# An encoder trunk on one core: the build orders its instructions by a timeline simulation in place of simple clocks

## The chip, the core and the metric

The kernel runs on one core of a Trainium2 chip. A core has five engines that each take a list of instructions in order: PE (TensorE, matrix multiplications; the loads of its weights are shown apart as PEld), DVE (VectorE), ACT (ScalarE), POOL (GpSimd) and SP (SyncE). Here SP does nothing but issue DMAs, the loads from memory into the core; POOL issues most stores and a few loads and does little else. An engine waits on semaphores for the others. The metric is the device time of one execution in microseconds.

## What is computed

The reference is one inference step of a trunk of two layers on 1024 new frames of one stream (the prompt) and 16 frames of each of 8 running streams (the sample), together T = 1152 tokens of width 1024. Layer 0 mixes with stick-breaking attention (8 heads of 64) beside a gated depthwise convolution of width 31; layer 1 mixes with attention over a band of chunks with a learned relative bias. Each layer ends in an MLP with a squared ReLU. All is in 32-bit floats.

```python
# layer 0, mixer (prompt; the sample also has cached k, v and u)
q, k, v, a, g = split(rmsnorm(x, g1) @ w_in)
u = a * sigmoid(g)
z = einsum(q, k) * HEAD_DIM ** -0.5
log_keep = where(mask, log_sigmoid(-z), 0)
between = cumsum(log_keep, reverse=True) - log_keep
w = where(mask, exp(log_sigmoid(z) + between), 0)
c = silu(layernorm(depthwise_conv(u, dw_w) + dw_b))
x = x + concat(w @ v, c) @ w_out
# layer 1, mixer
x = x + softmax(q @ k * scale + bias, in band) @ v @ w_out
# both layers
x = x + square(relu(rmsnorm(x, g2) @ w_up)) @ w_down
```

The outputs are the last layer's normed x, the new keys and values of both layers, and the last 30 rows of u.

## The kernel before

Activations lie transposed, channels on the partitions: a tile is 128 channels by tokens, the width 1024 is KC = 8 such tiles, and the tokens go through PE in three groups of G = 384 (the third holds the last 256 prompt tokens and the 128 of the sample). A 32-bit product is made of three matmuls: each operand is split into a high part, rounded by ACT (L180), and a low part, the rest, by DVE (L181), and high·high, high·low and low·high are summed (SPLIT, in `dense`, L208 to L222, whose matmul is L220). `load_split` (L190) loads 512 columns of a weight into a staging tile (`staging`, L185 to L187, tag st, three buffers) and splits it.

PE's results go to 8 banks of PSUM. The names of tiles in the order and in the trace follow the code: f20 is the bank of gate or value weight 2 and token group 0.

**Start** (`start`, within L674 to L806). The gate and value weights of the first two convolution chunks, numbered 0 to 3 (wf00 to wf31: weight, half), the tokens (x00 to x21: group, piece) and the states of the convolution (u0, u1, L631) are loaded on SP's queue. `ready` splits the weights (hl_wf for weights 0 and 1, hf for 2 and 3), `halves` the tokens (h0, L1543 and L1544), `squares` sums their squares (accs, L291 and L294), ones-matmuls of these (ms_h, L258) and a diagonal matmul (rr_h, L280) bring the row scale of the norm, and `sums` makes the banks f00 to f32. DVE's evacuations L636, L638 and L651 gate them into u0 to u3. The projections of q, k and v follow, whose weights are staged as st_wi; the cached keys of the sample come as ct00k to ct03k (L474).

**Mixer of layer 0.** For each pair of heads q, k, v are projected (psp, psa, psg), then for each block of queries scores z (L864 to L867), on ACT their exponentials, on DVE the reverse cumulative product (kp, L847, a scan along the keys) and its product with the gates (sg, L849), transposes on PE (tpa, L392), splits of these (wha on ACT, wla on DVE), products with v (ava, L404) and a sum (cpa, L414) that is stored to a buffer in memory, cat_d (L361). The sample's streams have the same steps with names in zs, kps, sgs. The convolution is 31 taps (`tap`, L655 to L675) for each of four chunks of channels, on DVE: y = u·w + y, one instruction for the prompt's 1024 tokens and one for the sample's 128; the last tap writes u, which goes to cat_d (L674, L675). The taps are steps of their own that a function `level` spreads between the attention's. `conv_norm` (L935) then loads that back as yl (L955, on POOL's queue), takes the mean by a matmul (mu, L961), subtracts it (L963) and normalizes. The output projection (psoa) follows per 128 channels (wo0a), with the residual in xo, stored as xm_d (L1028).

**MLP.** Up: um (L1380), squared ReLU (L1386 to L1390), stored as hid_d; down: hidden tiles are loaded as hrm, split (hsm), multiplied (pd, L1485), and added on DVE to sl (L1489). **Mixer of layer 1** runs pair by pair of heads: psc (L220), tpc (L392), avc (L404), psoa.

What sets the order: the Python code calls the instructions in an order that `merge` and `level` make from lists of steps with costs written into the code. The build then collects them and its scheduler decides the list of each engine anew, within the dependences; a few are tied by hand (taps come only after the weights step last named, L664). By default the scheduler keeps one simple clock for each engine.

```python
    with tile.TileContext(nc) as tc:
        tile_trunk(tc, ins, outs)
```

## Time and profile before

| | us |
|---|---|
| median of 3 runs | 2881.78 (2876.07 to 2883.00) |
| profiled execution | 2879.29 |
| its span on the core | 2877.5 |
| mean granted PE clock in it | 0.987 |

The span is the time from the first to the last instruction on the core. Times in the traces are us from its start. The stages lie at about: start 0 to 68, mixer of layer 0 to 474, convolution norm and output projection to 667, MLP to 1405, mixer of layer 1 to 1940, its end to 2110, MLP and final norm to 2877.

In a row of a timeline stand start, time taken, engine, line, operation, tile written and tiles read, and in brackets how long the engine had been idle and what ended that. In a row of a stage table stand the stretch, its length, the busy time of each engine with its number of instructions, the granted clock of PE as a share of full speed, the mean share of the core's DMA engines in use and GB/s.

### The profile page before, as it was taken

The page shows a single profiled execution, that of the slowest core. Times are in us where ns is not written, and L with a number is a line of the kernel's source. Part 1 is how long each engine was busy: PE and PEld are TensorE (multiplying, and loading weights), DVE is VectorE, ACT ScalarE, POOL GpSimd, SP SyncE. Part 2 cuts the span into 40 slices and gives each one's busy share as a digit, 9 for nine tenths or more (in the row PEclk, how much of TensorE's full clock was granted, in tenths as well). Part 3 has the DMA queues.
Part 4 walks back from the last instruction along what each step waited for, and adds up shares of the span by engine and source line. Part 5 has one row for each costly group of instructions (what it writes and reads, how often), then busy time and mean ns, then how long its engine had stood idle before and what let it go on. Part 6 is the DMA issues. An engine that isn't in the chain of part 4 may idle for free.

```text
span 2877.5 us, 48092 instructions
## 1 busy us (share of the span) xinstructions
PE 2778.7 (97%) x18586; PEld 2674.3 (93%) x18586; DVE 2015.6 (70%) x3939; ACT 1264.4 (44%) x2644; POOL 282.3 (10%) x511
## 2 busy tenths in 40 slices
PE   8988988899999999999999999998999999999998
PEld 8987876799999999999999999997999999999998
DVE  8999999988666654444567777778786666644445
ACT  5344446665555531211355555556555554411112
POOL 1000101031000000000111111110310110000001
PEclk9999998999999999999999999999999999999999
DMA  4434346443332362321344444446532322732311
GB/s 152 131 102 127 114 123 205 147 162 117 106 105 94 131 232 77 109 79 46 107 141 133 135 143 139 134 132 220 180 123 94 102 99 102 251 102 67 110 34 66
DMA packets 136004, 357.70 MB, mean 124 GB/s; under 512 B 21232, under 2 KB 44976, under 8 KB 133728
## 3 DMA queue, kind: packets, MB, share of 16 engines
q1 hardware_dynamic: 105936, 252.06, 27.5%
q0 software_dynamic: 29696, 102.56, 10.5%
q8 instruction: 146, 2.39, 0.3%
q14 instruction: 82, 0.67, 0.1%
q10 hardware_dynamic: 144, 0.02, 0.0%
HBM read 252.90 MB, written 89.03 MB: 119 GB/s over the span
## 4 chain that ended last, share of the span: by engine, by line
PE 75%; DVE 16%; ACT 4%; issue 3%; DMA 2%; POOL 0%; DVEq 0%; SPq 0%; ACTq 0%; POOLq 0%
PE pd L1485 28%; PE um L1380 23%; PE psc L220 10%; DVE y L671 4%; DVE kp L847 2%; PE avc L404 2%; PE psoa L220 2%; PE tpc L392 2%; PE f L220 1%; DVE sg L849 1%; PE zc L1137 1%; DVE wla L181 1%; PE zc L1138 1%; PE psp L220 1%; PE zs L505 1%
## 5 line engine op out<-in xcount | busy, mean ns | idle before, releaser
L1489 DVE TENSOR_TENSOR sl<-sl,pd 128x384 f32<-128x384 f32 x384 | 211.6, 552 | 342.4 <-PE pd L1485 342.0
L220 PE MATMUL psc<-h,hl_wc 128*128 128x384 f32 x1728 | 328.2, 340 | 0.0
L220 PEld LDWEIGHTS psc<-h,hl_wc 128*128 128x128 f32 x1728 | 298.5, 189 | 13.4 <-issue 11.5
L1380 PE MATMUL um<-sl,hl_m 128*128 128x288 f32 x1548 | 240.3, 296 | 0.0
L1380 PEld LDWEIGHTS um<-sl,hl_m 128*128 128x128 f32 x1548 | 217.7, 188 | 0.0
L671 DVE SCALAR_TENSOR_TENSOR y<-u,dw,y 128x1024 f32<-128x1024 f32 (+1 forms) x232 | 176.4, 807 | 0.4
L220 PE MATMUL psp<-h,hl_wi 128*128 128x384 f32 x864 | 169.7, 345 | 0.2 <-ACT kps L896 0.2
L220 PEld LDWEIGHTS psp<-h,hl_wi 128*128 128x128 f32 x864 | 150.4, 191 | 6.4 <-issue 4.9
L1485 PE MATMUL pd<-hsm,wdm 128*128 128x384 f32 x864 | 150.8, 334 | 0.0
L1485 PEld LDWEIGHTS pd<-hsm,wdm 128*128 128x128 f32 x864 | 149.9, 188 | 0.0
L181 DVE TENSOR_TENSOR hl_m<-xr,hl_m 128x512 fp32r<-128x512 f32 x132 | 92.4, 700 | 57.1 <-ACT hl_m L180 55.8
L180 ACT ACTIVATE hl_m<-xr 128x512 fp32r<-128x512 f32 x132 | 82.2, 623 | 104.7 <-PE um L1380 83.2
L1387 ACT ACTIVATE hdm<-hdm 128x288 f32<-128x288 f32 x192 | 84.8, 442 | 91.7 <-DVE hdm L1386 90.9
L1380 PE MATMUL um<-sl,hl 128*128 128x288 f32 x756 | 119.4, 296 | 0.0
L1104 ACT ACTIVATE s<-s,mxc 128x640 f32<-128x640 f32 (+4 forms) x128 | 88.8, 694 | 59.8 <-DVE mxc L1101 58.1
L1380 PEld LDWEIGHTS um<-sl,hl 128*128 128x128 f32 x756 | 106.6, 188 | 0.8
L180 ACT ACTIVATE wdm<-st_wd 128x512 fp32r<-128x512 f32 x40 | 23.8, 624 | 171.2 <-PE pd L1485 144.8
L1101 DVE CUSTOM_DVE_ANT_0 s<-zc,bp 128x384 f32<-128x384 f32 (+3 forms) x128 | 66.0, 517 | 38.9 <-PE zc L1138 38.1
L180 ACT ACTIVATE whc<-tpc 128x512 fp32r<-128x512 f32 (+1 forms) x144 | 72.5, 523 | 47.0 <-PE tpc L392 46.1
L181 DVE TENSOR_TENSOR wlc<-tpc,whc 128x512 fp32r<-128x512 f32 (+1 forms) x144 | 83.5, 595 | 12.8 <-ACT whc L180 10.4
L1390 POOL DMA_DIRECT2D hid_d<-hdm x96 | 51.9, 540 | 412.9 <-ACT hdm L1388 334.7
L180 ACT ACTIVATE hl<-st_wd 128x512 fp32r<-128x512 f32 x20 | 12.6, 629 | 171.0 <-PE pd L1485 155.3
(495 smaller groups left out, 6997.6 us busy)
## 6 DMA issues: line engine op xcount, KB each, us to landing
hrm<-hid_d SPq DMA_DIRECT2D x64, 576.0 KB, 5.0
xr<-in_w_up_dram SPq DMA_DIRECT2D x64, 512.0 KB, 3.7
st_wd<-in_w_down_dram SPq DMA_DIRECT2D x128, 256.0 KB, 3.3
hid_d<-hdm POOLq DMA_DIRECT2D x96, 288.0 KB, 2.4
st_wc<-in_w_in_c_dram SPq DMA_DIRECT2D x48, 256.0 KB, 2.7
xm_d<-xo POOLq DMA_DIRECT2D x16, 576.0 KB, 3.5
xr<-xm_d SPq DMA_DIRECT2D x16, 576.0 KB, 4.6
xr_d<-xr POOLq DMA_DIRECT2D x16, 576.0 KB, 3.3
```

The source lines that it names most:

```text
L180: ACT(hi, src, AF.Copy)
L181: return tt(lo, src, f(hi), ALU.subtract)
L220: mm(ps()[:, :G], hl[:, a, at:at + P], act[g][k // 4][b][:, k % 4, :], start=n == 0, stop=n == len(todo) - 1)
L392: nc.tensor.transpose(tp[:, c0 + q * P:c0 + (q + 1) * P], blocks.get(j, tile_q), ident)
L404: mm(st["av"][:, o0:o0 + n], vs[:, j, i].rearrange("p a d -> p (a d)"), src[:, c0:c0 + n], start=st["done"] == 0, stop=st["done"] == nmm - 1)
L671: stt(src if j == CW - 1 else dst, src, wj, dst, ALU.mult, ALU.add)
L1101: nc.vector.tensor_tensor_reduce(s[:, c:c + m], z, b, -1.0, mx, ALU.add, ALU.min, new)
L1104: ACT(s[:, :n], s[:, :n], AF.Exp, bias=mx, scale=-1.0, accum_out=tot)
L1380: mm(banks[b, n][:, :TQ], w[:, a, c * P:c * P + P], combo(key, c)[:, h, n * TQ:n * TQ + TQ], start=k < 3 and c == 0 and i == 0, stop=c == ...
L1387: ACT(y, y, AF.Relu)
L1485: mm(ps[:, :G], w[:, a, c % 4 * P:c % 4 * P + P], hid[NB * j + e][b][:, g * G:g * G + G], start=n == 0, stop=n == 3 * NB - 1)
L1489: tt(xs, xs, ps[:, :G], ALU.add)
```

## The change

The context in which the kernel is built gets a flag. The kernel's code, its tiles, buffers and pools stay as they are.

```diff
-    with tile.TileContext(nc) as tc:
+    with tile.TileContext(nc, schedule_with_timeline_sim=True) as tc:
         tile_trunk(tc, ins, outs)
```

With it the scheduler of the build ranks instructions by a simulation of the whole timeline. The two builds hold the same instructions on each engine; the lists differ in order, and with the order in which waits stand. Of the instructions before, 4928 of 17753 stand elsewhere among their neighbours on PE, 2418 of 3941 on DVE, 1246 of 2503 on ACT, 142 of 516 on POOL and 235 of 599 on SP. In the middle of both MLPs PE's list is the same.

The first place is SP's list at the program's start. Before:

```order
L187 DMA st_wf11_194<-in_w_in_ab_dram 128x512
L187 DMA st_wf20_196<-in_w_in_ab_dram 128x512
L698 DMA x10_229<-in_x_dram 128x768
L698 DMA x11_289<-in_x_dram 128x1152
L187 DMA st_wf21_231<-in_w_in_ab_dram 128x512
L698 DMA x12_291<-in_x_dram 128x1152
L187 DMA st_wf30_330<-in_w_in_ab_dram 128x512
L187 DMA st_wf31_332<-in_w_in_ab_dram 128x512
L698 DMA x20_350<-in_x_dram 128x1920
```

and, behind x21, u0, u1, st_wi4_0, st_wi4_1 and st_wi5_0, the cached keys ct00k00 to ct00k02. With the change, behind the same st_wf11 and x10 to x20:

```order
L698 DMA x21_352<-in_x_dram 128x1152
L631 DMA u0_382<-in_conv_in_dram 128x8x30
L631 DMA u1_389<-in_conv_in_dram 128x8x30
L474 DMA ct00k00_1145<-in_sb_k_dram 128x4x256
L474 DMA ct00k01_1147<-in_sb_k_dram 128x4x256
L474 DMA ct00k02_1149<-in_sb_k_dram 128x4x256
L187 DMA st_wf20_196<-in_w_in_ab_dram 128x512
L187 DMA st_wf21_231<-in_w_in_ab_dram 128x512
L187 DMA st_wf30_330<-in_w_in_ab_dram 128x512
L187 DMA st_wf31_332<-in_w_in_ab_dram 128x512
L187 DMA st_wi4_0_662<-in_w_in_ab_dram 128x512
```

Seven weight loads of 256 KB have moved behind ten loads of tokens, states and keys. PE's list at that place, where f20 is the first bank that needs st_wf20 (split as hf20), reads with the change:

```order
L220 MATMUL f10_233<-h0_70_190,hl_wf11_201 128x384
L220 MATMUL f20_264<-h0_00_159,hf20_258 128x384
L220 MATMUL f20_264<-h0_01_160,hf20_258 128x384
L258 MATMUL ms_h00_316<-ones_74,accs_140 128x1 x3
L220 MATMUL f01_354<-h0_00_159,hl_wf00_156 128x384
L220 MATMUL f01_354<-h0_01_160,hl_wf00_156 128x384
```

Before, all 24 matmuls of f20 stood ahead of ms_h00 and of f01; two of them still do.

The second place is DVE's list around kp100, the first scan of a head of the second pair, in the mixer of layer 0. Before:

```order
L671 SCALAR_TENSOR_TENSOR y2_2348<-u2_1429,dw_77,y2_2348 128x1024
L671 SCALAR_TENSOR_TENSOR y2_2348<-u2_1429,dw_77,y2_2348 128x128
L671 SCALAR_TENSOR_TENSOR y2_2348<-u2_1429,dw_77,y2_2348 128x1024
L671 SCALAR_TENSOR_TENSOR y2_2348<-u2_1429,dw_77,y2_2348 128x128
L414 TENSOR_TENSOR cpa013_2495<-ava013_2388,ata013_2493 64x256
L847 SCALAR_TENSOR_TENSOR kp100_2499<-kp100_2499,ones_74 128x128
```

With the change:

```order
L671 SCALAR_TENSOR_TENSOR u1_389<-u1_389,dw_77,y1_1236 128x1024
L671 SCALAR_TENSOR_TENSOR u1_389<-u1_389,dw_77,y1_1236 128x8x16
L181 TENSOR_TENSOR hl_wi14_0_2578<-st_wi14_0_2576,hl_wi14_0_2578 128x512
L847 SCALAR_TENSOR_TENSOR kp100_2499<-kp100_2499,ones_74 128x128
L668 TENSOR_SCALAR y2_2348<-u2_1429,dw_77,cvec_78 128x1024
L668 TENSOR_SCALAR y2_2348<-u2_1429,dw_77,cvec_78 128x128
```

The first nine pairs of taps of chunk 2, which stood ahead of that scan, now stand behind it: u1's last tap comes just before the scan. Taps lag behind the attention's steps like this from the start of the mixer, by up to about 13 us of tap work, and have caught up at the last scan, kps30.

The third place is POOL's list at the end of the taps, where the last chunk's result u3 goes to cat_d and yl is loaded from there. Before:

```order
L361 DMA cat_d0_109<-cpa202_4248 64x256
L674 DMA cat_d0_109<-u3_2647 128x1024
L675 DMA cat_d0_109<-u3_2647 128x8x16
L361 DMA cat_d0_109<-cpa203_4420 64x256
L819 DMA out_sb_v_dram<-sv03_4306 128x1152
L361 DMA cat_d0_109<-cpa210_4502 64x256
L955 DMA yl00_4667<-cat_d0_109 128x384
L350 DMA l0_745<-l0_745 64x1024
L955 DMA yl01_4668<-cat_d0_109 128x384
```

With the change:

```order
L361 DMA cat_d0_109<-cpa211_4570 64x256
L347 DMA k1_744<-k1_744 64x1024
L350 DMA l1_746<-l1_746 64x1024
L674 DMA cat_d0_109<-u3_2647 128x1024
L675 DMA cat_d0_109<-u3_2647 128x8x16
L361 DMA cat_d0_109<-cpa212_4644 64x256
L955 DMA yl00_4667<-cat_d0_109 128x384
L955 DMA yl01_4668<-cat_d0_109 128x384
L955 DMA yl02_4669<-cat_d0_109 128x384
```

The store of u3 has moved behind four more of the attention's stores and stands right ahead of the yl loads, which depend on it. On DVE u3's last tap has moved with it, from just ahead of the scan kp212 to behind sg217, the last scan of that head, near the end of the stage. At the turn from up to down in the MLPs, SP's list has hidden tiles hrm and pieces of sl ahead of the down weights st_wd, and PE's first down rows (pd) go through seven banks with the first hidden tile before the second tile comes; before, the first bank took the first four tiles before the second bank was opened.

## The prediction

> **What bounds the kernel now.** I read the page first, then a table of busy time by stage, then the waits of PE and DVE inside the stages that are not full, then the timelines around the places where the order differs. The page says how much there is to gain at all:
>
> ```profile
> span 2877.5 us, 48092 instructions
> ...
> PE 2778.7 (97%) x18586; PEld 2674.3 (93%) x18586; DVE 2015.6 (70%) x3939; ACT 1264.4 (44%) x2644; POOL 282.3 (10%) x511
> ...
> PE 75%; DVE 16%; ACT 4%; issue 3%; DMA 2%; POOL 0%; DVEq 0%; SPq 0%; ACTq 0%; POOLq 0%
> ```
>
> The change removes no instruction, so PE's 2778.7 us of matmuls stay. PE is idle for 2877.5 − 2778.7 = 98.8 us, and no order can give back more. The stages show where that idle lies (columns: stretch in us, its length, then busy us of PE, PEld, DVE, ACT and POOL, the granted clock, the DMA share and GB/s):
>
> ```profile
> core 0: us, PE busy (x) PEld busy (x) DVE busy (x) ACT busy (x) POOL busy (x), PEclk, DMA share, GB/s
> 16.00:28.00 12.00, 10.42 (x61) 9.86 (x60) 11.15 (x29) 11.30 (x24) 0.00 (x0) 1.00 0.98 319
> 50.00:68.00 18.00, 18.00 (x95) 17.74 (x94) 15.23 (x28) 6.11 (x14) 1.47 (x2) 0.91 0.24 66
> 68.00:108.00 40.00, 40.00 (x234) 39.97 (x233) 39.81 (x49) 10.42 (x19) 4.65 (x8) 1.00 0.29 76
> 108.00:474.00 366.00, 327.60 (x2316) 283.92 (x2314) 357.19 (x498) 170.28 (x386) 35.64 (x63) 0.95 0.44 131
> 474.00:600.00 126.00, 111.05 (x753) 95.16 (x753) 112.83 (x210) 88.07 (x193) 11.88 (x20) 0.96 0.50 171
> 667.00:1009.00 342.00, 342.00 (x2577) 342.00 (x2576) 231.65 (x447) 180.73 (x391) 33.51 (x62) 1.00 0.32 110
> 1430.00:1940.00 510.00, 501.47 (x3649) 474.63 (x3649) 364.80 (x1014) 269.28 (x618) 62.42 (x144) 1.00 0.44 135
> ```
>
> The first MLP (667 to 1009 is its up half) is full of matmuls; its order on PE changes only at its ends, so it can neither gain nor lose. From 50 to 108 PE is full too. From 108 to 474, the stick-breaking mixer with the convolution beside it, DVE is the bound: 357.2 of 366 us, 8.8 idle, while PE waits 38.4. From 474 to 600 neither is full (PE idle 15.0, DVE 13.2): chains of short steps. The second mixer (1430 to 1940) has 8.5 us of PE idle in 510. So the order can matter in the first 50 us, in the DVE-bound stage, and at the seams.
>
> **The first term: the third and fourth gate weights come later.** The order shows that on SP's list the loads of st_wf20, st_wf21, st_wf30, st_wf31 and the first three st_wi move behind the tokens x10 to x21, the convolution states u0 and u1, and three 512-KB key-cache loads ct00k. Before, SP ran them so:
>
> ```profile
> 9.13 0.33 SPq L187 DMA_DIRECT2D st_wf<-in_w_in_ab_dram  x1
> ...
> 13.38 0.84 SPq L187 DMA_DIRECT2D st_wf<-in_w_in_ab_dram  x2
> ...
> 20.16 5.00 SPq L187 DMA_DIRECT2D st_wi<-in_w_in_ab_dram  x3
> 25.20 1.53 SPq L474 DMA_DIRECT2D ct00k<-in_sb_k_dram  x3
> ```
>
> The two landing rows below are for the st_wf20 issued at 9.13 and for the three ct00k issued from 25.20:
>
> ```profile
> DMA to landing us min/median/max: 3.3/3.3/3.3
> DMA to landing us min/median/max: 4.8/5.7/6.5
> ```
>
> st_wf20 landed at 9.13 + 3.3 = 12.4. The last ct00k was issued at about 26.2 and landed 6.5 later, at 32.7. In the changed order that ct00k is without the seven weight loads ahead of it: 7 × 0.262 MB = 1.84 MB, which at the 319 GB/s of the stretch 16 to 28 (DMA share 0.98, so the transfers themselves are the limit there) is 5.8 us. It lands at about 27.0, and st_wf20, the next 0.262 MB, at 27.8. I take it that what stands later in SP's list lands later.
>
> ```profile
> L180 ACT ACTIVATE hf<-st_wf x4: 615/617/633, 12.5 to 21.0; 128x512 fp32r<-128x512 f32 x4
> 16.50 4.33 PE L220 MATMUL f<-h,hf 128*128 128x384 f32 x24
> 27.27 0.91 PE L280 MATMUL rr_h<-accs,ones 128*128 128x384 f32 x2 [1.58 <-DVE accs L276]
> 49.29 0.62 PE L220 MATMUL f<-h,hl_wf 128*128 128x384 f32 x2 [1.79 <-ACT h L180]
> 50.30:52.60 2.30, 2.30 (x7) 0.51 0.00 0
> ```
>
> ACT splits the weight in 0.62 us, so the matmuls f20, which began at 16.50, can begin at 28.4: 11.9 us of stall. Before, the cover was 16.50 − 12.4 − 0.6 = 3.5 us; all of it goes. PE's new list has two f20 matmuls right behind f10, ahead of the sums ms_h00 and of the f01 group that needs only weights already here, so nothing passes the blocked matmul. Off this come the 1.58 us that PE waited at 27.27 for the row scale rr_h: its chain of short DVE and ACT steps goes on once ACT has split st_wf31 (three loads behind st_wf20, so landed at about 30.3) and ends at about 35, an estimate, before PE arrives there at about 39. The wait at 49.29 stays: its chain follows PE's own rr_h. After the stall comes a slow start: the stretch 50.30 to 52.60, behind a wait of 1.79 us, ran at a granted clock of 0.51, and 2.30 × 0.49 = 1.1 us were lost; I add 1.1. The sum is 11.9 − 1.6 + 1.1 = 11.4.
>
> [...]
>
> Nothing gives this back before 108: PE is full from 50 on, and DVE's taps, which fill it from 62, wait for u0, which PE's f02 makes. DVE idles 18.00 − 15.23 = 2.8 us from 50 to 68, of which a part may go because ACT has had time to split weights early. I take 11 for the start; the bounds are 8 (st_wf20 lands 3 us sooner because bytes of several loads move side by side) and 13.5.
>
> **The second term: taps later in the DVE-bound stage.** DVE's list now runs the depthwise-convolution taps behind the attention's steps: at the scan kp100, nine of chunk 2's tap pairs stood ahead of it, now none. By the timeline a pair takes 1.5 us, so that scan stands some 13 us earlier among DVE's work. At the end of the stage (the scan kps30 at 474.5) the lag is zero. PE's waits that could shrink:
>
> ```profile
> PE ava L404 <- DVE wla L181: 13.2, 14, 2.5
> PE tpa L392 <- DVE sg L849: 7.7, 9, 1.9
> DVE yl L963 <- PE mu L961: 3.0, 1, 3.0
> ```
>
> But DVE has the same work to do until kps30, and a PE that waits less only waits elsewhere for the bound. What the stage can yield is DVE's own idle, 8.8 us; of that half is realistic, −4, mostly the 3.0 before yl. Against it stands the last chunk's store, which moves with its taps:
>
> ```profile
> 434.12 1.53 DVE L671 SCALAR_TENSOR_TENSOR u<-u,dw,y 128x1024 f32<-128x1024 f32 x2
> 435.70 0.56 POOL L674 DMA_DIRECT2D cat_d<-u  x1 [13.12 <-DVE u L671]
> ...
> 444.16 2.16 POOL L955 DMA_DIRECT2D yl<-cat_d  x4
> 464.14 2.85 PE L961 MATMUL mu<-yl,ones 128*128 128x384 f32 x8
> cat_d<-u POOLq DMA_DIRECT2D x4, 512.0 KB, 3.8
> yl<-cat_d POOLq DMA_DIRECT2D x12, 192.0 KB, 3.7
> ```
>
> By DVE's new list u3's last tap comes some 27 us of DVE work later, at about 461.5 on the old clock. Store 1.2 to issue and 3.8 to land, reload 1.4 and 3.7: yl03 is there at about 471.6, where PE's mu0 now stands at about 469 to 471 in PE's own order. Before, mu0 had some 15 us of cover; now it has none, and PE, with psoa and zs queued behind it, and DVE, whose yl step waits for mu0, stand for 1 to 6 us. I take +4. Middle: 0, with bounds −8 (all DVE idle back, no wait at mu0) and +7.
>
> **The seams.** At the turn from up to down in each MLP, PE's list now opens the output banks with the first hidden tile before it goes on to the second, and SP loads hidden tiles and the residual ahead of the down weights. Before:
>
> ```profile
> 1011.37 8.88 PE L1485 MATMUL pd<-hsm,hl_wd 128*128 128x384 f32 x49 [0.69 <-DVE hsm L181]
> ```
>
> That 0.69 goes, and each tile is needed about 8 us later, but is also loaded about 8 us later; 0 to +2 for each of two turns, I take +1 for both. From 474 to 600 and in the pairs of the second mixer PE's rows are reordered by a few steps around the same chains: ±3 each, 0 taken. At the second mixer's end
>
> ```profile
> 1950.30 1.54 PE L392 MATMUL tpc<-ident,s 128*128 128x128 f32 x6 [3.25 <-DVE s L1106]
> ```
>
> goes (the rows ahead of it fill it), but the output projection behind it stands up to 4.6 us closer to the DVE and ACT steps that feed it: between −3 and +6, I take 0. The sum: 11 + 0 + 1 + 0 = **+12** on the profiled execution's 2879.3 us (span 2877.5 and 1.8 around it). The median shown is 2881.8, 2.5 above; I forecast on the profiled footing, **2891 us**.
>
> **Rivals.**
> - *The loss at the start is paid back in part.* The DVE-bound stage gives up 4 to 8 of its 8.8 us and mu0 does not wait, or st_wf20 lands 3 us sooner. For it: 13 us less tap work ahead of the scans. Against: DVE has only that idle to give. 2880 to 2887.
> - *Faster.* Place: 108 to 600. If DVE's list lets about 13 us of its work fall behind the point that PE needs at 474, into the 13.2 us that DVE idles from 474 to 600, then DVE no longer bounds the mixer and PE takes back 13 and another 8 of its waits of 13.2 and 7.7 us: 2879.3 + 11 − 21 = 2869. It decides from 20 us on. Against: the lag is zero at kps30 and the convolution's norm needs the taps.
> - *Slower still.* Scans that stand 10 us earlier in DVE's list wait there for ACT and PE, who feed them; with mu0's 6 us and both turns at +2: 11 + 6 + 4 + 4 = 25, or 2904.
> - *Nothing comes of it.* The late weights are made up while PE waits for DVE anyway: 2879 to 2882. Against: the taps cannot start before u0, and so shift with PE.
>
> **How the numbers follow.** My forecast (2887 to 2899) gets 0.45, the part payment 0.27, slower still 0.13, faster 0.09, nothing 0.06. A measurement of this kernel can tell about 0.3%, 8.6 us, from no change. Faster by more is the one case, 0.09; within it are the part payment and nothing, 0.33; slower by more is the rest, 0.58. The range of 2878 to 2905 takes in all but the faster case and the tail of the slower one.
>
> **What would show it.** In the changed trace PE's f20 group should begin near 28.4 after about 12 us of idle on a DMA of st_wf, and f02 near 60.5; mu0 should show a wait on a POOL load of yl near 480; DVE's idle from u0 to kps30 should stay between 3 and 10 us; both MLPs should keep their length. If f20 begins before 22, the first term is wrong; if PE's waits between 108 and 474 shrink by more than 10 us with an earlier kps30, the second is.

## The result, and the profile after

| | before | changed |
|---|---|---|
| median | 2882.39 us (2876.07 to 2886.45, 4 runs) | 2920.93 us (2918.23 to 2923.33, 4 runs) |
| ratio | | 1.0135, 95% interval 1.012 to 1.015 |
| span of the profiled execution | 2877.5 us | 2921.5 us |
| mean granted PE clock | 0.987 | 0.978 |

The kernel became slower by 1.35%, some 39 us, where +12 was forecast; the time lies 16 us above the end of the range. The first rows of the page after, those that answer to the page before:

```profile
span 2921.5 us, 48152 instructions
...
PE 2795.5 (96%) x18586; PEld 2692.6 (92%) x18586; DVE 2019.2 (69%) x3939; ACT 1261.1 (43%) x2644; POOL 284.7 (10%) x511
...
PE 76%; DVE 15%; ACT 3%; issue 3%; DMA 2%; DVEq 0%; SPq 0%; ACTq 0%
```

The work is the same. PE's idle grew from 98.8 to 126.0 us, and its busy time by 16.8. (These two executions lie 44 us apart, five more than the medians.) The stages, cut at the same instructions as before (columns as in the table before):

```profile
16.00:28.00 12.00, 3.71 (x21) 3.39 (x20) 12.00 (x30) 11.00 (x24) 0.00 (x0) 0.80 0.90 280
66.30:84.30 18.00, 18.00 (x93) 18.00 (x92) 11.01 (x20) 3.41 (x8) 1.66 (x2) 0.87 0.24 66
84.30:124.30 40.00, 40.00 (x235) 39.97 (x234) 38.10 (x50) 10.42 (x19) 5.61 (x9) 1.00 0.33 84
124.30:501.40 377.10, 330.28 (x2316) 287.93 (x2313) 361.13 (x500) 171.93 (x389) 34.54 (x62) 0.92 0.43 129
501.40:629.00 127.60, 111.54 (x752) 97.45 (x753) 112.68 (x209) 87.49 (x190) 12.47 (x21) 0.95 0.48 161
700.00:1042.00 342.00, 342.00 (x2569) 341.20 (x2569) 227.50 (x448) 179.38 (x391) 33.54 (x62) 1.00 0.32 110
1461.00:1978.00 517.00, 505.53 (x3647) 476.31 (x3647) 365.95 (x1014) 269.21 (x617) 65.17 (x144) 1.00 0.43 133
```

In the first 12 us of the stall PE works 3.7 where it worked 10.4. The DVE-bound stage takes 377 us in place of 366, the second mixer 517 in place of 510, the first MLP's up half 342.0 in both. Since both kernels hold the same instructions, each can be matched with itself. The median of how much later PE starts an instruction than in the kernel before, by its time before:

```
stretch before   later by (us)
 68 to  108       16.3     behind the start
350 to  400        9.2     the mixer of layer 0, attention ahead of the taps
474 to  500       27.1     its end
560 to  600       29.1     convolution norm, output projection
700 to 1000       33.1     layer 0's MLP
1430 to 1500      31.0     first pairs of layer 1's mixer
1900 to 1940      38.1     its last pairs
2000 to 2040      42.2     its end
2200 to 2440      43.5     layer 1's MLP
2800 to 2850      43.1
```

So the loss comes in three places, and only the first was forecast: about 16 at the start, 11 at the end of layer 0's mixer, 11 in and behind layer 1's. The MLP start near 660 loses 4, the two turns to the down halves give back 1.1 and 0.4.

### The profile page after: what moved, and what is told of

Same layout as the page of the kernel before. It is cut to its first block, busy times and chain, and to the rows that moved or that the text cites. A ratio compares the mean times of both kernels' runs of the same rounds, so it can differ in the third digit from the quotient of the medians.

```text
span 2921.5 us, 48152 instructions
## 1 busy us (share of the span) xinstructions
PE 2795.5 (96%) x18586; PEld 2692.6 (92%) x18586; DVE 2019.2 (69%) x3939; ACT 1261.1 (43%) x2644; POOL 284.7 (10%) x511
## 3 DMA queue, kind: packets, MB, share of 16 engines
q0 software_dynamic: 29696, 102.56, 10.4%
## 4 chain that ended last, share of the span: by engine, by line
PE 76%; DVE 15%; ACT 3%; issue 3%; DMA 2%; DVEq 0%; SPq 0%; ACTq 0%
PE pd L1485 27%; PE um L1380 24%; PE psc L220 10%; DVE y L671 3%; PE psp L220 2%; DVE kp L847 2%; PE avc L404 2%; PE f L220 1%; PE psoa L220 1%; PE tpc L392 1%; DMA cr<-cat_d 1%; DVE sg L849 1%; PE zc L1138 1%; PE zc L1137 1%; DVE wla L181 1%
## 5 line engine op out<-in xcount | busy, mean ns | idle before, releaser
L220 PE MATMUL psc<-h,hl_wc 128*128 128x384 f32 x1728 | 344.9, 344 | 0.0
L220 PEld LDWEIGHTS psc<-h,hl_wc 128*128 128x128 f32 x1728 | 296.6, 189 | 12.6 <-issue 11.2
L220 PE MATMUL psp<-h,hl_wi 128*128 128x384 f32 x864 | 166.3, 342 | 1.2 <-ACT sw L527 0.7
L220 PEld LDWEIGHTS psp<-h,hl_wi 128*128 128x128 f32 x864 | 149.4, 190 | 5.8 <-issue 2.4
L180 ACT ACTIVATE hl_m<-xr 128x512 fp32r<-128x512 f32 x132 | 83.1, 630 | 138.7 <-PE um L1380 90.4
L847 DVE TENSOR_TENSOR_SCAN kp<-kp,ones 128x128 f32<-128x128 f32 (+3 forms) x64 | 86.4, 1350 | 1.8 <-ACT kp L869 1.5
L180 ACT ACTIVATE lo<-st_wd 128x512 fp32r<-128x512 f32 x30 | 18.0, 626 | 161.1 <-PE pd L1485 155.3
```

The lines of the kernel that those rows point to most:

```text
L180: ACT(hi, src, AF.Copy)
L220: mm(ps()[:, :G], hl[:, a, at:at + P], act[g][k // 4][b][:, k % 4, :], start=n == 0, stop=n == len(todo) - 1)
L847: nc.vector.tensor_tensor_scan(keep[:, 0:n][:, ::-1], keep[:, 0:n][:, ::-1], ones[:, 0:1].to_broadcast([P, n]), 1.0, ALU.mult, ALU.mult)
```

## The experiments

Most runs mix the two orders. The kernel is built once with the other scheduler, the order of each engine's list is read from that build, and in the build that runs, neighbours in that list are tied in that order for chosen engines and chosen parts of the program. Nothing is computed otherwise. What a rule does not name, the scheduler orders anew around the tied lists, so that a run can move more than its rule says; where that matters, the traces below show it. The edit against the kernel before, shown once, shortened at `...` and with comments for the reader (a later diff gives only its rules and which scheduler runs; FLAG True is the simulated one, and `order_of` reads the lists of a build):

```diff
+MARKS = []      # counts of traced instructions: 0 begin, 1 end of start(), 2 last pair of
+                # layer 0, 3 end of its mixer, 4 and 5 layer 1's mixer, 6 end
+def tie(tc, order, rules):
+    have = {i.name: (k, i) for k, i in enumerate(tc.nc.cur_bb.bb.instructions)}
+    info = mybir.DependencyInfo(mybir.DependencyClass.NoSync, mybir.DependencyReason.DATA)
+    for engine, lo, hi in rules:
+        seq = [have[n] for n in order[engine] if MARKS[lo] <= have[n][0] < MARKS[hi]]
+        for (_, a), (_, b) in zip(seq, seq[1:]):
+            tc.add_manual_dep(b, a.name, info, reason="order")
...
-    with tile.TileContext(nc) as tc:
-        tile_trunk(tc, ins, outs)
+    nc = build(FLAG, (order_of(*build(not FLAG)), RULES))[0]
```

### The three places, one at a time

**start_only** is the order before with the start from the simulated order.

```diff
+    FLAG, RULES = False, [(e, 0, 1) for e in (PE, DVE, ACT, POOL)] + [(SP, 0, 2)]
```

> The order before everywhere but in the start, which is tied to the simulated order (SP's loads up to the last pair of layer 0 too). Theory (the start's loss goes through to the end undiminished): 2882 + 16 = 2898, ratio 1.0055. By the sum of the prediction: 2882 + 11 = 2893, ratio 1.004. Rival (absorbed): 2882 to 2886.

Ratio 1.0062 (1.0047 to 1.0077), 2899.2 us against 2881.6: +17.6. The start costs what the trace of the changed kernel shows, and it goes through to the end.

**start_back** is the reverse: simulated order, the start tied to the order before.

```diff
+    FLAG, RULES = True, [(e, 0, 1) for e in (PE, DVE, ACT, POOL)] + [(SP, 0, 2)]
```

> Simulated order everywhere but in the start: what start() traces (and SP's loads up to the last pair of layer 0) is tied, engine by engine, to the order before. Theory (the start's loss of 16.3 us, read where PE is full at 68 to 108, lies on the path to the end because DVE is full behind it): 2921 - 16 = 2905, ratio to before about 1.008. Rival (the mixer of layer 0 absorbs it, since PE waits there anyway): 2915 to 2921, ratio 1.012 or more. By the sum of the prediction (11.4 us): 2910.

Ratio 1.0109 (1.0094 to 1.0124): only some 9 of the 16 to 18 us came back, between theory and rival; that the sum of the prediction had said 2910 is luck, for the start alone costs 17.6. The timelines of PE, ACT and DVE show where part of the rest went. The tie ends where the next part begins, and there PE's list puts 19 matmuls of the next projection (psp) among those that the last gate of u0 needs, on which in turn the taps wait; before, none stood there. ACT waits 4.74 us for PE where it waited 1.45, and the gate comes at 65.59, 5.4 later than before.

```profile
59.08 1.20 PE L220 MATMUL psp<-h,hl_wi 128*128 128x384 f32 x6
61.16 2.41 PE L220 MATMUL psp<-h,hl_wi 128*128 128x384 f32 x13
64.48 0.55 ACT L634 ACTIVATE u<-f 128x256 f32<-128x256 f32 x2 [4.74 <-PE f L220]
65.59 0.62 DVE L651 TENSOR_TENSOR u<-f,u 128x256 f32<-128x256 f32 x2 [4.97 <-ACT hl_wi L180]
```

**mid_only** is the order before with the rest of layer 0's mixer, from the start's end, in simulated order.

```diff
+    FLAG, RULES = False, [(e, 1, 3) for e in (PE, DVE, ACT, POOL, SP)]
```

> The order before, but everything traced from the end of the start to the end of layer 0's mixer is tied to the simulated order on all engines. Theory (start and middle add up: 17.6 for the start alone, 28 for both by the run with the whole mixer tied back): 2882 + 10 = 2892, ratio 1.0035. Rival (the middle loses only because it comes in late and out of step behind the slow start; alone it gains the 2 to 6 us that PE's rows show in it before 440): 2876 to 2880.

Ratio 1.0045 (1.0030 to 1.0060), +13. With nothing late ahead of it, PE's instructions stand 8.1 us earlier at 350 to 400 by the median, and 9.1 later at 474 to 500: the lead is given back and more, in the last 60 us.

**mixer0_back** ties the whole of layer 0's mixer back.

```diff
+    FLAG, RULES = True, [(e, 0, 3) for e in (PE, DVE, ACT, POOL, SP)]
```

> Simulated order, but all of layer 0's mixer (start, four pairs, convolution norm, output projection) tied to the order before on all engines. Theory (by the traces 29 of the 43 us arise before 640, the rest in layer 0's MLP start and in layer 1): 2921 - 27 = 2894, ratio 1.004 to 1.005. Rival (start and middle pay each other back in part, as with only the start tied, which gave 9.4 of 16): 2900 or more.

Ratio 1.0039 (1.0024 to 1.0054): 27 to 28 of the 39 us are start and middle together, which agrees with 17.6 and 13 alone within their intervals. No seam is left between them here.

**mix1_back** and **mix1_only** do the same with the mixer of layer 1.

```diff
+    FLAG, RULES = True, [(e, 4, 5) for e in (PE, DVE, ACT, POOL, SP)]     # mix1_back
+    FLAG, RULES = False, [(e, 4, 5) for e in (PE, DVE, ACT, POOL, SP)]    # mix1_only
```

> Simulated order everywhere but in the mixer of layer 1, tied to the order before. Theory (that stage loses 7 us in its pairs, about 4 by finer switching between kinds of matmul and 3 by waits for ACT's split whc, and 4 more behind the last pair): 2921 - 11 = 2910. Rival (switching costs nothing, only the waits come back): 2921 - 4 to 6 = 2916.

> The order before, with the mixer of layer 1 alone tied to the simulated order on all engines. Theory (that stage costs 10.3 us wherever it starts, as in the run with it alone tied back): 2882 + 10 = 2892, with 98 first matmuls of projections at 0.26 us where the order before has 57, and the waits for whc. Rival (it costs only in a kernel that is late elsewhere): 2882 to 2885.

mix1_back: 1.0102 (1.0087 to 1.0117), 10.3 us less than the changed kernel. mix1_only: 1.0046 (1.0027 to 1.0064), +13; some 3 of these arise near 660, ahead of the mixer, where that profile has a slow start of PE, and 10 in it. The stage costs 10 us wherever it starts.

### What holds PE at the start

**late_loads** ties SP's loads alone. **start_split** ties the lists of PE, DVE, ACT and POOL alone.

```diff
+    FLAG, RULES = False, [(SP, 0, 2)]                                     # late_loads
+    FLAG, RULES = False, [(e, 0, 1) for e in (PE, DVE, ACT, POOL)]        # start_split
```

> The order before on every engine but SP, whose loads up to the last pair of layer 0 are tied to the simulated order: st_wf20 to st_wi5_0 behind the tokens, states and keys. Theory (the late weights alone cost what the prediction summed, 11.4 us, and the other 5 of the start come from DVE's and PE's order): 2882 + 11 = 2893. Rival (the loads cost it all, or more, since ACT's and DVE's old lists now block at hf20 ahead of the next tokens): 2898 or more.

> The order before everywhere but in the start on PE, DVE, ACT and POOL, tied to the simulated order; SP's loads stay as before, so the weights are there in time. Theory (the rest of the start's loss: DVE scales all eight tiles of the last token group ahead of their low parts, so PE waits 2.65 us behind the first three matmuls of f02, and starts slowly again): 2882 + 5 = 2887. Rival (nothing without the late loads): 2882. Rival (the order costs it all, the loads nothing): 2898.

late_loads: 1.0039 (1.0024 to 1.0054), +11.2, the prediction's sum of 11.4. start_split: 1.0042 (1.0027 to 1.0057), +12, where 5 was expected. Neither run moved only what its rule names. In start_split SP's list was a new one, and the weights were not on time as expected: st_wf20 landed at 17.7, where it landed at 12.5 before, at 26.7 in late_loads and at 26.0 in the changed kernel. In late_loads ACT's list too had put its squares ahead of hf20. PE's timelines at f20 of late_loads, start_split and the changed kernel, in this order:

```profile
27.77 1.01 PE L220 MATMUL f<-h,hf 128*128 128x384 f32 x2 [11.31 <-ACT hf L180]
```

```profile
25.89 1.01 PE L220 MATMUL f<-h,hf 128*128 128x384 f32 x2 [7.39 <-ACT hf L180]
```

```profile
27.46 1.01 PE L220 MATMUL f<-h,hf 128*128 128x384 f32 x2 [8.29 <-ACT hf L180]
65.63 1.65 PE L220 MATMUL f<-h,hl_wf 128*128 128x384 f32 x4 [2.65 <-DVE h L181]
```

ACT's timelines at the split of st_wf20, in the same order:

```profile
27.11 1.66 ACT L180 ACTIVATE hf<-st_wf 128x512 fp32r<-128x512 f32 x3
25.23 1.66 ACT L180 ACTIVATE hf<-st_wf 128x512 fp32r<-128x512 f32 x3
26.79 1.66 ACT L180 ACTIVATE hf<-st_wf 128x512 fp32r<-128x512 f32 x3
```

f20 is held twice. In none of the three rows did ACT wait: it came to the split from its squares. In start_split the weight had been there for 7.5 us, and f20 still waits until 25.89, because ACT's simulated list splits the next tokens and takes their squares ahead of hf20. In late_loads the load alone, at 26.7, would have held f20 to 27.3. A trace that names the late load, or ACT, shows only the one that opened last. With both, in the changed kernel, f20 begins 11.0 later than before (27.46 against 16.50) and PE stands 16.3 later behind the start; what the start costs beyond 11 stands behind f20. The 2.65 in the last row is a third cost: DVE's list scales all eight tiles of the last token group before it makes the first low part, where the list before went three and three. A fourth is the granted clock, below.

### What is lost in the middle

kps20 and kps30 are the scans of the sample's streams in the third and the fourth pair of heads; kps30 ends the DVE-bound stage. Less DVE's idle until then, kps30 starts at 453 to 455 us in each of these orders: the work that DVE has ahead of it is the same.

```
kernel       DVE idle before kps20   from kps20 to kps30   kps30 starts   start less idle
before             16.7                    4.8                474.5           453.1
changed            35.3                   12.3                501.9           454.3
start_only         32.1                    4.4                489.5           453.0
mid_only           17.2                   12.1                483.9           454.6
last_back          34.8                    9.5                498.3           454.0
taps_first         41.7                   11.8                508.4           454.9
mid_back           27.4                    4.7                485.0           452.9
mid_pe_back        44.1                   10.9                509.2           454.2
mid_dve_back       41.6                    7.2                502.1           453.3
```

What is left to explain is where DVE waits. In the changed kernel, the 7.5 us by which the second column differs stand behind the last taps. DVE's, PE's and POOL's timelines there:

```profile
486.86 1.50 DVE L181 TENSOR_TENSOR cat<-cr,cat 128x384 fp32r<-128x384 f32 x3 [2.75 <-ACT cat L180]
492.32 1.25 DVE L181 TENSOR_TENSOR wla<-tpa,wha 128x512 fp32r<-128x512 f32 x2 [3.96 <-ACT wha L180]
496.20 1.95 DVE L963 SCALAR_TENSOR_TENSOR yl<-mu,yl 128x384 f32<-128x384 f32 x4 [2.63 <-PE mu L961]
```

```profile
476.61 1.10 PE L220 MATMUL psoa<-cat,hl_wo0a 128*128 128x384 f32 x2 [5.02 <-ACT cat L180]
486.88 2.38 PE L220 MATMUL psoa<-cat,hl_wo0a 128*128 128x384 f32 x6 [5.03 <-ACT cat L180]
```

```profile
482.38 0.55 POOL L674 DMA_DIRECT2D cat_d<-u  x1 [10.14 <-DVE u L671]
488.78 1.60 POOL L955 DMA_DIRECT2D yl<-cat_d  x3 [3.31 <-DMA cat_d<-u]
```

u3's store and the reload of yl come at 482 and 489, close behind each other as forecast, and DVE then waits 2.6 for mu0. But psoa on PE, and the splits cat on ACT and DVE, also stand ahead of the last steps of the attention and wait for the reload cr, and those steps wait behind them, with no taps left to fill DVE.

**last_back** ties only the last pair's part back. **taps_first** keeps the simulated order and holds each scan behind the tap traced last ahead of it.

```diff
+    FLAG, RULES = True, [(e, 2, 3) for e in (PE, DVE, ACT, POOL, SP)]     # last_back
...
+                            done["tap"] = stt(src if j == CW - 1 else dst, src, wj, dst, ALU.mult, ALU.add)
...
+                with tc.issue_after(done["tap"].ins):                     # taps_first
                     nc.vector.tensor_tensor_scan(keep[:, 0:n][:, ::-1], keep[:, 0:n][:, ::-1],
```

> Simulated order everywhere but in the last pair of heads of layer 0 with the taps left, the convolution norm and the output projection, which are tied to the order before. Theory (DVE's total work bounds that stage, so only DVE's idle behind the last tap can come back, 10.7 us there against 4.5 before): 2921 - 6 to 10, so 2911 to 2915. Rival (the whole step from +10 to +27 us that PE's instructions show between 440 and 500 is lost by the order of this stage): 2921 - 17 = 2904.

> Simulated order, and one more rule: each scan of the stick-breaking weights is issued behind the tap traced last ahead of it, so the taps stand at the scans as in the order before. Theory (the late taps make the last chunk's store, its reload yl and the mean mu0 late, and DVE idles 12.3 us from 382 to kps30 where it idled 4.7): 2921 - 7 = 2914. Rival (the waits there come from PE's list, where psoa stands ahead of its loads, not from the taps): 2919 to 2921. Rival (taps as filler were worth the 6 us that PE's instructions gain from 108 to 400, and these go too): 2920 to 2926.

last_back: 1.0136 (1.0119 to 1.0153), no gain that can be told; the theory of 6 to 10 us failed. taps_first: 1.0144 (1.0127 to 1.0161), if anything slower. DVE's timelines of last_back and of taps_first show the wait that each left:

```profile
490.86 1.49 DVE L966 SCALAR_TENSOR_TENSOR yl<-mu,yl 128x384 f32<-128x384 f32 x3 [4.54 <-PE mu L964]
```

```profile
499.33 0.56 DVE L181 TENSOR_TENSOR cat<-cr,cat 128x384 fp32r<-128x384 f32 x1 [8.19 <-ACT cat L180]
```

With the waits for cat gone, mu0 costs 4.5; with the taps early, the split cat costs 8.2. In taps_first DVE's idle ahead of kps20 also grows by 6.4, which fits taps that had filled the time behind the scans.

**mid_back** ties everything from the start's end to the mixer's end back, so that both waits go.

```diff
+    FLAG, RULES = True, [(e, 1, 3) for e in (PE, DVE, ACT, POOL, SP)]
```

> Simulated order, but everything traced from the end of the start to the end of layer 0's mixer tied to the order before on all engines. Two waits stand at the end of that part in the changed kernel: the late taps (store of u3, reload yl, mean mu0) and the early place of the split cat and of psoa ahead of the reload cr. The run with the last pair alone tied back took away the second, the run with the taps tied to the scans the first, and neither gained. Theory (each wait covers the other, and with both gone the middle's price comes back): 2921 - 11 = 2910. Rival (the price is that of being late after the slow start and cannot come back): 2918 or more.

Ratio 1.0085 (1.0071 to 1.0099), 14 us less than the changed kernel. The table divides it: kps30 comes 16.9 earlier, 7.6 of DVE's idle from the end of the stage, where it is down to 4.7, and 7.9 from the start, since the tie of SP's list, which begins with the key loads, pulled st_wf20 forward too (f20 starts at 22.07). So the total alone would not decide, but the column does: the end's loss of 7.5 us of idle comes back whole when both waits go, and 2.8 and 0.5 of it when one does.

**mid_pe_back**, **mid_dve_back** and **mix1_pe_back** tie single engines.

```diff
+    FLAG, RULES = True, [(PE, 1, 3)]                                      # mid_pe_back
+    FLAG, RULES = True, [(DVE, 1, 3), (ACT, 1, 3)]                        # mid_dve_back
+    FLAG, RULES = True, [(PE, 4, 5)]                                      # mix1_pe_back
```

> Simulated order, but PE's list for what is traced from the end of the start to the end of layer 0's mixer is tied to the order before (the scheduler fits the other engines' lists to it). Theory (psoa stands too early on PE's list and blocks the last attention steps, 5.0 us twice, while DVE runs dry): 2921 - 8 = 2913. Rival (it is DVE's and ACT's lists): 2919 to 2923.

> The same with DVE's and ACT's lists tied to the order before in that part, and PE's left to the simulation. Theory (on DVE the split of the last keys, which frees the buffer that the reload cr00 takes, stands 18 us later than before, behind taps, and so come cr, cat and psoa): 2921 - 8 = 2913. Rival (PE's list): 2919 to 2923.

> Simulated order, but PE's list in layer 1's mixer is tied to the order before. Theory (the loss there, 10.3 us by the run with all engines tied back, is PE's list: finer switching and avc ahead of its whc): 2921 - 10 = 2911. Rival (ACT's and DVE's lists bring the splits whc late): 2917 to 2921.

1.0185 (1.0170 to 1.0200), 1.0142 (1.0127 to 1.0157) and 1.0167 (1.0150 to 1.0184): no faster than the changed kernel, the first clearly slower, the last just so. All three theories failed. Here one engine's list of one schedule did not fit the others' of the other, so the loss cannot be handed to one engine this way.

### The places that gain

**turns_only** takes the down halves of both MLPs from the simulated order, with a mark at each turn.

```diff
+        MARKS.append(len(nc.cur_bb.bb.instructions))
         for i in range(NB):
             down_w(i)
...
+    FLAG, RULES = False, [(e, a, b) for a, b in ((4, 5), (7, 8)) for e in (PE, DVE, ACT, POOL, SP)]
```

> The order before, with the down halves of both MLPs alone tied to the simulated order on all engines: the only places where the changed kernel's rows gain on those before (1.1 and 0.4 us, 1.4 in other runs). Theory (a gain of 1 to 3 us, near the bound of what can be told): 2879 to 2881. Rival (nothing, or the late hidden tiles wait): 2882 to 2884.

Ratio 0.9991, interval 0.9981 to 1.0000: 2878.5 against 2882.4. A gain of this size is at the edge of what can be told, and not established.

## Why the prediction was right or wrong

**What bounds the kernel: right, but PE's 2778.7 us did not stay.** In the changed kernel too DVE is busy in 361 of the 377 us of its stage, with the same work ahead of kps30 in nine orders, and both MLPs kept their length. But the prediction took PE's busy time as fixed by its instructions and only the 98.8 us of idle as open, and with the same instructions PE was busy 16.8 us longer. By the clock records of the two traces 90.4 us of its work fell into stretches at half the clock, where it was 57.2; half of the difference is 16.6 us (by the median a matmul of 128x384, L220, took 0.33 us at the full clock and 0.52 at the half, and was followed by the next one 0.17 and 0.32 us later). (The second mixer's 4.1, below, come on top, and where as much was saved was not looked for.)

**The late loads: right, and not the whole start.** f20 was put at 28.4 and began at 27.46, which is 11.0 later than before, against 11.9 in the sum; st_wf20 landed at 26.0 where 27.8 was put. late_loads cost 11.2 against 11.4. That ACT's new list held f20 as well was not seen, though the list was in hand; in the changed kernel it decided less than 1 us. The start measures 17.6, not 11, and two terms failed, both behind f20. The wait of 2.65 for the low parts of the last token group was put at nothing, since they were not looked at. The slow start was put at 1.1. That was read from a stretch of 2.30 us, and the half clock lasted longer; before, then changed:

```profile
50.30:53.70 3.40, 3.40 (x11) 3.40 (x12) 3.40 (x8) 1.57 (x3) 0.00 (x0) 0.50 0.00 0
```

```profile
23.20:33.50 10.30, 6.04 (x21) 6.04 (x22) 8.99 (x24) 6.71 (x12) 0.00 (x0) 0.50 0.58 192
64.20:71.10 6.90, 5.47 (x17) 5.47 (x18) 4.66 (x10) 1.46 (x3) 0.00 (x0) 0.51 0.00 0
```

PE worked 11.5 us at the half clock where it worked 3.4: half of the difference, 4 us, was lost.

**The DVE-bound stage: the failed step is the offset of -4 against +4.** The wait for mu0 was there. The -4, half of DVE's idle, did not come: it rested on the thought that critical steps which stand earlier must help. They did stand earlier, by 8 us in mid_only, but the work of DVE until kps30 was the same, as the prediction itself said, and what the early part left over was the taps, without which the last steps had no filler. The price measured is +13 with the output projection (mid_only), 9.4 of it at kps30, and not 0. The early place of psoa and cat was visible in PE's and ACT's lists. Of the signs named, DVE's idle from u0 to kps30 failed: 17.9 us, where 3 to 10 were named and 9.1 were there before. The wait at mu0 showed on DVE; PE itself had other work in it.

**Layer 1's mixer: the failed step is "reordered by a few steps around the same chains", taken as 0 within 3.** It cost 10. PE waited longer, in short pieces; the waits of PE there, before and changed:

```profile
PE avc L404 <- ACT whc L180: 5.7, 5, 1.1
PE tpc L392 <- DVE s L1106: 2.6, 6, 0.7
```

```profile
PE avc L404 <- ACT whc L180: 11.5, 17, 1.0
```

That is 11.5 against 8.3, +3. By the stage rows busy time grew by another 4.1, at a granted clock of 1.00 in both. An order that repeats once a pair costs its price eight times: about 1 us a pair was the loss, and a bound of 3 for the whole stage was one for a single place. What lies behind the last pair, 4 us more, was inside the bounds given (-3 to +6).

**The MLP start near 660** lost 4 in the changed kernel and was left out of the prediction's sum. From 690 to 700 the granted clock was 0.72; PE's longest waits ahead of that stretch, back to 620, were of 2.70 and 0.67 us.

```profile
690.00:700.00 10.00, 10.00 (x57) 10.00 (x58) 8.66 (x30) 2.79 (x8) 0.00 (x0) 0.72 0.36 129
```

**The rivals.** The direction was right: slower by more than 0.3% had 0.58. "Slower still" came nearest, at 2904 with a chance of 0.13; it named mu0 and the turns, of which mu0 was one of two waits and the turns gained.

**What stays open.** Why layer 1's lists cost 10 is read from the traces, with the price of a switch below; no run changed the switches alone. mix1_pe_back brought their number back to 57, and PE's waits in that stage grew to 16.3 us. The 3 to 4 us near 660 appeared in several mixes and were not tried by themselves. Nor was the clock: that its loss follows from more and longer waits is the author's reading of two traces in which both grew, PE's idle from 98.8 to 126.0 us and its work at half the clock from 57.2 to 90.4. Each trace is of one execution.

## What to carry to other kernels

Where a new order holds an instruction in more than one way, removing one hold can show nothing: look in every list that feeds it, and undo holds together. Work that only fills gaps is worth most where the last serial chain runs, so an order that uses it up, or starts that chain late, pays at the end what it gained on the way. A loss of 1 us in a part that repeats is to be multiplied before it is called small. PE's busy time was not fixed by its instructions here: with the same ones it grew by 16.8 us, and its work at half the clock from 57.2 to 90.4 us.

## What the runs showed of the hardware

The first projection matmul (128x384, operands rounded, in the kernel's F32R tiles, L220) behind a matmul on plain 32-bit operands (transposes L392, and L505, L510, L547 and the like) was followed by its neighbour 0.26 to 0.28 us later in place of 0.174, in each such place: 57 of 57 in layer 1's mixer before, 98 of 98 in the changed kernel, whose list mixes the kinds more finely (the one place behind L280 in each, 0.47 us, not counted). Behind other rounded matmuls (L404, L1138) it took 0.17 to 0.24 us, in none of 60 and 58 places as long. The 41 places more at some 0.085 us are 3.5 of the 4.1 us by which PE's busy time grew there.

In the stretch below, at the end of layer 0's mixer in the changed kernel, PE's granted clock was 0.50; no wait of PE in it was longer than 1.57 us, and none in the 6 us ahead of it was longer than 1.41.

```profile
456.70:467.00 10.30, 6.74 (x23) 5.21 (x24) 10.24 (x12) 3.18 (x6) 0.54 (x1) 0.50 0.04 9
```

In the clock records of the two traces the half clock came in 13 stretches before and 20 in the changed kernel, and each lasted 3.4, 6.8 or 10.2 us (the last, at the end of the trace, left out). By the row 50.30 to 53.70 above, where PE was busy for all of 3.40 us at 0.50, such a stretch of 3.4 us costs it 1.7 us, an estimate (3.40 × 0.50). No run tried one wait by itself.
